# A list-scheduled trunk kernel: a re-ordered opening, later softplus, and a list model with shared ports and earlier loads

## The chip, the cores and the metric

The kernel runs on one core of a Trainium2 chip. The metric is the device time of one execution in microseconds (us); three executions of the kernel before took 1260.82, 1262.92 and 1263.37 us, the median is 1262.92 us.

## What is computed

Two layers (`DEPTH` 2) work on 256 tokens of width 1024. Cut to what matters here:

```python
for l in range(DEPTH):
    mod = silu(c) @ w_ada[l] + b_ada[l]                 # 6 * 1024 modulation values
    h = rms_norm(x, norm1_g[l]) * (1 + sc1) + sh1       # needs the first 2 * 1024 of them
    proj = h @ w_in[l]       # q, k, v, iq, ik, iw, z, xbc, dt_raw, ga, gm: 10856 columns
    o_attn = dsa_attention(rope(norm(q)), rope(norm(k)), v, rope(iq), rope(ik), iw) @ w_attn_o[l]
    dt = softplus(dt_raw + dt_bias[l])                  # one value per token and head (256 x 32)
    y = ssd_scan(silu(conv(xbc)), dt, a_log[l])
    x = x + g1 * ((sigmoid(ga) * o_attn + sigmoid(gm) * (norm(y * silu(z)) @ w_ssm_o[l])) @ w_out[l])
    x = x + g2 * conv_ffn(rms_norm(x, norm2_g[l]) * (1 + sc2) + sh2)
```

All of it is in float32. A weight product is made of three fp32r products: each weight slab is split into a rounded part `wh` and a rest `wl`, each activation into two parts in the same way.

## The kernel before, in words

**Slabs and splits.** Weights come as slabs of 4 x 128 rows by 512 columns (1 MB), loaded through the SP queue into three buffers (`st`, tag `wst`). `split_now` makes `wh` on ScalarE (ACT) and `wl = st - wh` on VectorE (DVE). A chunk of 512 output columns over 1024 rows needs two slabs. TensorE (PE) works through the chunks in the order of `plan`; between groups of products it calls `pump` (each call counts one in `slabs`), which enters small tasks from the lists `hot`, `warm`, `calm` and `cool`: the transposes, ropes, softplus, attention, scan. A task says how many pumps it waits (`later(n, ...)`) or for which tiles (`Need`).

**The static order.** Every instruction is written down once, in a fixed order for each engine, by a planner inside `trunk`. PE instructions are placed as the program comes to them, at a clock `now` that `on_pe` advances by modelled durations. Instructions of DVE, ACT, GpSimd (POOL) and the loads are entered with `give` as `Work` with a modelled duration (`takes`), and `plan_ahead` simulates all queues and picks for each engine the work that could start first (among those ready, the one entered first; `urgent` moves work ahead). `commit` then issues what starts before `now - LEAD_IN`. The modelled times decide the order only: on the chip each engine runs its list in order and waits for what it needs. In the model a load takes its bytes at 300 bytes/ns and is seen 2500 ns after its end (`HOP["dma"]`).

**Ports in the model.** A DVE `tensor_tensor` with all operands in SBUF and at least 128 elements is `heavy`: while one runs, a POOL instruction progresses at 0.18 of its speed (`CROWD`). DVE itself is never slowed.

**The opening** (`run_open`). Before layer 0 can start, the first 2048 modulation values are needed. They are made in four quarters `q`, each from two slabs of `w_ada` (`ada`, 1 MB each, five buffers of pool `op`). `ada_products` multiplies a slab with the replicated silu(c) (16 products, 32 PE instructions). Then `open_mod` runs the chain of the quarter: ACT copies the sums (`adarow`), PE transposes them, DVE adds the bias (`mod`, `amul`), and `norm_tile` makes two activation tiles `h` (DVE, ACT, DVE). With these and the quarter's slab of `w_in` four **fills** (`weigh`) can run: products for the columns of iq and k, and with two of them the narrow `misc` columns (ik, iw, dt). `modulations` is a generator that yields a `Need` ahead of each step; the loop at the end of `run_open` runs fills while the needed tile is not there by the plan's clock, but starts none within `FILL` (300 ns) of it. `warm_up(n)` writes n products of two tiles of ones into a bank that nobody reads: 10 ahead of the first modulation products, 8 after the first quarter's chain. `tables` makes the rope tables (about 25 small DVE instructions and 4 Sin on ACT) after the chain of quarter 1.

**After the opening** come the chunks Q0, V0, K1, Q1, V1, two of B and C, then the scan's inputs. The four banks of pool `pj` hold two chunks; a chunk's first product waits until its banks were read by the rope or the copy of the chunk two before.

**Softplus** (`dt_task`, in `use_misc`). When `misc` has been turned, some 26 small DVE instructions (128x64 elements) and an Exp make dt = softplus(...). The task goes to `hot` at once, and all instructions up to the polynomial's start are entered in one step. `ssd` needs its result about eight chunks later.

The queries below name line L190 for nearly everything: all instructions are issued from that one line of `commit`, so tiles tell them apart.

Of the kernel before, what the change touches and what calls it, by code (L numbers as in the profile page):

```python
# [46 lines left out]
def trunk(ctx, tc, x, c, positions, w_ada, b_ada, norm1_g, w_in, q_norm_g, k_norm_g, ssm_conv_w, ssm_conv_b,  # L47
# [13 lines left out]
    CROWD = 0.18  # L61
    ORDER = ("dve", "act", "pool", "dma", "dma_act", "dma_pool")
# [5 lines left out]
    class Work:  # L68


        __slots__ = ("key", "ns", "pr", "deps", "least", "start", "end", "done", "issue", "heavy")

        def __init__(self, key, ns, deps, least, issue):
            number[0] += 1
            self.key, self.ns, self.pr, self.deps, self.least = key, ns, number[0] - boost[0], deps, least
            self.start, self.end, self.done, self.issue, self.heavy = None, None, False, issue, False
# [36 lines left out]
    crowd_done = [0.0]  # L113

    def crowded(t, ns, until):

        if until <= t:
            return t + ns
        part = CROWD * (until - t)
        return t + ns / CROWD if ns <= part else until + ns - part  # L120

    def plan_ahead():
# [6 lines left out]
        crowd, slow = crowd_done[0], None  # L129
# [3 lines left out]
        while todo:  # L133
            best = None
            for key, ws in todo.items():
                first = None
                for w in ws[:1] if key == "dma" else ws:
                    t = w.least
                    for d in w.deps:
# [4 lines left out]
                        e += (HOP[key] if d.key[:3] != "dma" else HOP["dma"]) if d.key != key else -LAP["act"] if key == "act" else 0.0  # L144
# [5 lines left out]
                    if first is None or t < first[0]:  # L150
# [22 lines left out]
    def commit(edge=None):  # L173
# [3 lines left out]
        for key, ws in waiting.items():  # L177
            for w in sorted(ws, key=lambda w: w.start):
                if w.start < edge:
# [3 lines left out]
                    if w.heavy:  # L183
                        crowd_done[0] = w.end
# [3 lines left out]
        n = 0  # L188
# [6 lines left out]
    def end_of(w, by=None):  # L195
        if not w.done:
            plan_ahead()
        return w.end + (HOP["dma"] if w.key[:3] == "dma" else HOP[by] if by else 54.0)
# [90 lines left out]
    def give(key, outs, ins, ns, issue, least=None, heavy=False):  # L289
        deps = needs_of(outs, ins) + [w for w in behind_of if w.key == key]  # L290
        w = Work(key, ns, deps, now[0] - LEAD_IN if least is None else least, issue)
        w.heavy = heavy
# [18 lines left out]

    class Timed:
# [5 lines left out]
        def __getattr__(self, name):  # L318
            fn = getattr(self.eng, name)

            def call(*a, **k):
# [6 lines left out]
                if name.startswith(("affine", "memset")):  # L328
                    return give(self.key, outs, ins, 100.0 + 0.4 * outs[0].free_size(), issue)
                heavy = (self.key == "dve" and name == "tensor_tensor" and outs[0].free_size() >= 128  # L330
                         and not any(x.tensor._space == PSUM for x in outs + ins))
                return give(self.key, outs, ins, takes(self.key, name, outs, ins, k), issue, heavy=heavy)
# [1470 lines left out]
```

## Time and profile before

| | |
|---|---|
| median of three executions | 1262.92 us |
| the profiled execution | 1262.23 us, its span from first to last instruction 1260.5 us |
| PE busy | 1225.6 us, 97% of the span |
| DVE / ACT / POOL busy | 956.3 / 762.2 / 414.3 us |
| mean granted TensorE clock | 0.989 of 2.4 GHz |
| chain that ended last | PE 79%, DVE 12%, ACT 4%, "issue" 3%, POOL 2% |
| HBM read | 243.9 MB, 194 GB/s over the span |

Busy time of PE counts a matmul until its modelled end, and matmuls overlap, so a stretch that is busy throughout can still hold short waits. The idle time of PE and the granted clock (1.00 is 2.4 GHz, 0.50 is 1.2 GHz) tell what a stretch loses at least.

### The profile page before, as it was taken

How to read it: one execution, taken by the hardware profiler on the slowest of the kernel's cores; microseconds unless marked ns; L12 is line 12 of the kernel's file. 1: busy time of each engine (PE TensorE's matmuls, PEld its weight loads, DVE VectorE, ACT ScalarE, POOL GpSimd, SP SyncE). 2: the span in 40 equal slices, each digit the busy share in tenths (PEclk: the TensorE clock that was granted, in tenths of full speed). 3: DMA queues.
4: the chain of work that ended last, by engine and by line, in shares of the span. 5: the costliest groups of instructions: out<-in, count | busy, mean ns of one | idle time of the engine just before them, and what ended most of it. 6: DMA issues, size and time to landing. Idle time of an engine off the chain costs nothing.

```text
span 1260.5 us, 24567 instructions
## 1 busy us (share of the span) xinstructions
PE 1225.6 (97%) x9789; PEld 1140.5 (90%) x9789; DVE 956.3 (76%) x1477; ACT 762.2 (60%) x1362; POOL 414.3 (33%) x479
## 2 busy tenths in 40 slices
PE   7789999999999999999999999999999999999998
PEld 6577789999989999999997778999999999999998
DVE  4499977878786778889757997888777766678753
ACT  3356677774764357777436467877467544777742
POOL 2042533343262124564211443323304511335400
PEclk8889999999999999999989999999999999999999
DMA  9654644457456647876756455355764665566542
GB/s 300 231 182 144 209 146 171 163 193 255 159 203 215 234 156 239 276 248 229 247 180 201 148 195 193 126 170 172 240 204 153 215 236 166 181 209 202 195 162 73
DMA packets 158663, 246.53 MB, mean 196 GB/s; under 512 B 11868, under 2 KB 66870, under 8 KB 158549
## 3 DMA queue, kind: packets, MB, share of 16 engines
q1 hardware_dynamic: 157989, 244.77, 58.4%
q8 instruction: 77, 1.26, 0.4%
q14 instruction: 37, 0.30, 0.1%
q0 software_dynamic: 288, 0.19, 0.1%
q10 hardware_dynamic: 272, 0.00, 0.0%
HBM read 243.89 MB, written 1.05 MB: 194 GB/s over the span
## 4 chain that ended last, share of the span: by engine, by line
PE 79%; DVE 12%; ACT 4%; issue 3%; POOL 2%; DVEq 0%; POOLq 0%; ACTq 0%
PE bk L190 79%; DVE wl L190 4%; DVE w L190 1%; ACT wh L190 1%; DVE adacc L190 1%; DVE t L190 1%; DVE p L190 1%; POOL w L190 1%; ACT w L190 1%; ACT p L190 1%; DVE mx L190 1%; DVE ss L190 1%; DVE top L190 0%; POOL rows L190 0%; POOL rr L190 0%
## 5 line engine op out<-in xcount | busy, mean ns | idle before, releaser
L190 PE MATMUL bk<-h,wh 128*128 128x256 f32 x3488 | 646.8, 286 | 0.4 <-ACT h L190 0.4
L190 PEld LDWEIGHTS bk<-h,wh 128*128 128x128 f32 x3488 | 543.4, 192 | 12.1 <-issue 9.6
L190 DVE TENSOR_TENSOR wl<-st,wh 128x2048 fp32r<-128x2048 f32 (+1 forms) x200 | 435.0, 2179 | 146.4 <-ACT wh L190 146.0
L190 PE MATMUL bk<-h,wl 128*128 128x256 f32 x1744 | 492.0, 283 | 0.0
L190 ACT ACTIVATE wh<-st 128x2048 fp32r<-128x2048 f32 (+1 forms) x200 | 352.1, 1768 | 213.2 <-PE bk L190 176.7
L190 POOL TENSOR_TENSOR w<-w,w 128x254 f32<-128x254 f32 (+2 forms) x213 | 208.0, 992 | 416.1 <-DVE w L190 330.2
L190 PEld LDWEIGHTS bk<-h,wl 128*128 128x128 f32 x1744 | 334.1, 192 | 0.5
L190 PE MATMUL bk<-u,wh 128*128 128x256 f32 x1344 | 234.7, 279 | 0.0
L190 PEld LDWEIGHTS bk<-u,wh 128*128 128x128 f32 x1344 | 203.3, 188 | 1.6 <-issue 1.6
L190 PE MATMUL bk<-u,wl 128*128 128x256 f32 x672 | 186.1, 277 | 0.0
L190 PE MATMUL bk<-wh,h 128*128 128x512 f32 x448 | 150.4, 411 | 11.9 <-ACT wh L190 5.2
L190 ACT ACTIVATE w<-bk,vec 128x256 f32<-128x256 f32 (+2 forms) x272 | 122.2, 516 | 33.3 <-DVE w L190 19.6
L190 PEld LDWEIGHTS bk<-u,wl 128*128 128x128 f32 x672 | 126.2, 188 | 0.0
L190 DVE SCALAR_TENSOR_TENSOR adacc<-ad,chalf,adacc 128x512 f32<-128x512 f32 x140 | 121.6, 869 | 4.6 <-DMA ad<-in_w_ada_dram 4.0
L190 PEld LDWEIGHTS bk<-wh,h 128*128 128x128 f32 x448 | 83.8, 193 | 33.6 <-issue 8.0
L190 DVE SCALAR_TENSOR_TENSOR w<-bk,vec,w 128x255 f32<-128x255 f32 (+1 forms) x184 | 81.5, 475 | 16.4 <-ACT w L190 15.8
L190 PE MATMUL bk<-wl,h 128*128 128x512 f32 x224 | 90.4, 404 | 3.3 <-DVE wl L190 3.3
L190 POOL TENSOR_TENSOR u<-u,u 128x256 f32<-128x256 f32 (+1 forms) x56 | 67.3, 1219 | 57.4 <-ACT u L190 33.6
L190 POOL TENSOR_TENSOR rr<-ss,mhalf 128x16 f32<-128x16 f32 x8 | 26.0, 3254 | 98.3 <-DVE ss L190 98.3
L190 PEld LDWEIGHTS bk<-wl,h 128*128 128x128 f32 x224 | 43.4, 194 | 14.1 <-DVE wl L190 5.3
L190 ACT ACTIVATE w<-w 128x256 f32<-128x256 f32 x92 | 35.6, 412 | 30.3 <-POOL w L190 30.1
L190 ACT ACTIVATE u<-bk 128x128 f32<-128x128 f32 (+2 forms) x128 | 32.1, 325 | 30.7 <-PE bk L190 30.6
(194 smaller groups left out, 1178.5 us busy)
## 6 DMA issues: line engine op xcount, KB each, us to landing
st<-in_w_in_dram SPq DMA_DIRECT2D x80, 1024.0 KB, 5.1
st<-in_w_up_dram SPq DMA_DIRECT2D x88, 512.0 KB, 5.4
ad<-in_w_ada_dram SPq DMA_DIRECT2D x160, 256.0 KB, 5.4
st<-in_w_down_dram SPq DMA_DIRECT2D x20, 1024.0 KB, 5.3
st<-in_w_ssm_o_dram SPq DMA_DIRECT2D x16, 1024.0 KB, 5.3
st<-in_w_ada_dram SPq DMA_DIRECT2D x16, 512.0 KB, 10.2
st<-in_w_attn_o_dram SPq DMA_DIRECT2D x8, 1024.0 KB, 5.0
st<-in_w_out_dram SPq DMA_DIRECT2D x8, 1024.0 KB, 5.2
```

What stands on the lines that cost most here:

```text
L190: begun[n].issue()
```

## The change

- **The list model.** `heavy` becomes a pair `port` = (`share`, `soft`) from the new `port_of`: while a DVE instruction with `share` below 1 runs, a POOL `tensor_tensor` progresses at that share, and DVE's own end moves by `soft` times the overlap. `plan_ahead` prefers a work entered earlier if a later one would not start sooner by more than `PATIENCE` (0.2) of the later one's duration. A load is seen `EARLY` (1300 ns) after its end if that lies before 45 us, the rate is 330 instead of 300 bytes/ns up to 45 us, and the first load starts at 2.0 us. `on_pe` takes PE to be slow after a wait of over 2000 instead of 3000 ns.
- **The opening.** The two fixed `warm_up` calls go. `keep_warm(need)` puts unread products into each planned wait, ahead of fills and ahead of modulation products. Their bank is held for the whole opening. `FILL` becomes 700 ns. `tables` moves from after quarter 1's chain to after quarter 0's.
- **Softplus** is entered 44 pumps later, with more yields inside, in both layers.

```diff
+    PATIENCE = 0.2
+    EARLY = 1300.0
...
+    def landing(w):
+        return EARLY if w.end < 45000.0 else HOP["dma"]
...
-                    if first is None or t < first[0]:
+                    if first is None or t + PATIENCE * w.ns < first[0]:
...
-            if key == "pool":
-                w.end = crowded(t, w.ns, crowd)
-                slow = w
-            elif w.heavy:
-                crowd = w.end
-                if slow and slow.end > t:
-                    slow.end = crowded(t, slow.end - t, crowd)
-                    at["pool"] = max(at["pool"], slow.end - LAP["pool"])
+            if key == "pool" and w.share < 1.0:
+                w.end = crowded(t, w.ns, vec)
+                gps = w
+                if vec and not vec.done and vec.end > t:
+                    vec.end += vec.soft * (min(vec.end, w.end) - t)
+                    at["dve"] = max(at["dve"], vec.end - LAP["dve"])
+            elif key == "dve" and w.share < 1.0:
+                if gps and gps.end > t:
+                    w.end += w.soft * (min(w.end, gps.end) - t)
+                    if not gps.done:
+                        gps.end = crowded(t, gps.end - t, w)
+                        at["pool"] = max(at["pool"], gps.end - LAP["pool"])
+                vec = w
...
+    def port_of(key, name, outs, ins):
+        n = outs[0].free_size()
+        if key == "pool":
+            return (0.5, 0.0) if name == "tensor_tensor" and n >= 128 else (1.0, 0.0)
+        if key != "dve" or n < 128:
+            return 1.0, 0.0
+        if any(x.tensor._space == PSUM for x in outs + ins):
+            return 0.8, 0.0
+        if name == "tensor_tensor":
+            return 0.18, 0.1 if n > 1024 else 0.45
+        return (0.55, 0.45) if name == "scalar_tensor_tensor" else (1.0, 0.0)
...
-            give("dma", [out], [src], out.partition_size() * out.free_size() * 4 / (200.0 if now[0] < 1.0 else 300.0), issue, now[0] - 30000.0)
+            give("dma", [out], [src], out.partition_size() * out.free_size() * 4 / (250.0 if now[0] < 1.0 else 330.0 if now[0] < 45000.0 else 300.0), issue, max(2000.0, now[0] - 30000.0))
...
-        if ready > at + 3000.0:
+        if ready > at + 2000.0:
...
         misc = hold(bank())
+        spare["bank"] = hold(bank())
...
+        def keep_warm(need):
+            n = int((need.at() - now[0] - 300.0) / 225.0)
+            if n > 1:
+                warm_up(n)
...
                 if q == 1:
-                    for _ in tables():
-                        pass
                     ch["start"]()
...
                 if q == 0:
                     ahead(ch["m"], ch["m"] + 1)
-                    spare["bank"] = bank()
-                    warm_up(8)
+                if q == 0:
+                    for _ in tables():
+                        pass
...
-        warm_up(10)
         for need in modulations():
             while fills and fill_need(*fills[0]).at() < need.at() and now[0] < need.at() - FILL:
+                keep_warm(fill_need(*fills[0]))
                 fill()
+            keep_warm(need)
         ahead(ch["ada"][3][-1])
-        done(crep)
+        done(crep, spare["bank"])
...
-    FILL = 300.0
+    FILL = 700.0
...
+        DT_AFTER = 44
...
                 A.activation(e, e, AF.Exp)
+                yield
...
                 V.tensor_tensor(s2, d, d, op=ALU.mult)
+                yield
...
+                    if n % 4 == 1:
+                        yield
...
-            hot.append(dt_task())
+            hot.append(later(DT_AFTER, dt_task()))
```

## Rows read from the trace of the kernel before

**Rows 1.** The page's first part: busy us (share of the span), instructions.

```profile
PE 1225.6 (97%) x9789; PEld 1140.5 (90%) x9789; DVE 956.3 (76%) x1477; ACT 762.2 (60%) x1362; POOL 414.3 (33%) x479
```

**Rows 2.** Busy time by stretch: length, each engine (instructions), PEclk, DMA share, GB/s.

```profile
13.90:72.00 58.10, 46.76 (x412) 36.26 (x412) 27.91 (x83) 23.02 (x45) 3.95 (x13) 0.87 0.79 262
72.00:90.00 18.00, 14.42 (x60) 11.58 (x59) 17.64 (x32) 7.66 (x9) 10.39 (x5) 0.91 0.55 176
...
90.00:1260.50 1170.50, 1156.67 (x9284) 1086.39 (x9282) 904.65 (x1341) 725.82 (x1291) 391.79 (x412) 1.00 0.58 192
...
100.00:160.00 60.00, 58.66 (x350) 47.38 (x349) 58.93 (x132) 37.31 (x84) 27.03 (x25) 1.00 0.55 186
```

**Rows 3.** Waits of PE, 0 to 90 us: total us, times, longest.

```profile
PE bk L190 <- ACT wh L190: 5.2, 2, 4.1
PE bk L190 <- DVE sp_p L190: 3.6, 1, 3.6
PE bk L190 <- ACT h L190: 3.2, 2, 2.1
...
PE bk L190 <- DVE wl L190: 2.2, 3, 1.0
...
PE bk L190 <- ACT adarow L190: 0.8, 2, 0.4
```

**Rows 4.** Timeline of PE in the opening: start, us, what [idle before, releaser].

```profile
10.41 3.56 PE L190 MATMUL bk<-ones 128*128 128x128 f32 x20 [2.05 <-ACT bk L190]
...
17.08 1.95 PE L190 MATMUL bk<-ones 128*128 128x128 f32 x16
...
30.97 1.08 PE L190 MATMUL bk<-st,w 128*32 128x128 f32 x32
...
36.87 0.80 PE L190 MATMUL bk<-wh,h 128*128 128x512 f32 x1 [4.09 <-ACT wh L190]
...
58.13 1.08 PE L190 MATMUL bk<-st,w 128*32 128x128 f32 x32
...
62.00 0.50 PE L190 MATMUL bk<-wh,h 128*128 128x512 f32 x1 [2.06 <-ACT h L190]
```

**Rows 5.** One fill as a stretch; tile st's modulation loads (first, last issue) and landings.

```profile
53.43:55.29 1.86, 1.86 (x13) 1.58 (x10) 0.00 (x0) 0.00 (x0) 0.00 (x0) 1.00 0.93 330
...
L190 SPq DMA_DIRECT2D st<-in_w_ada_dram x16: 379/636/3612, 3.1 to 39.9; - x16
...
DMA to landing us min/median/max: 6.2/9.3/10.6
```

**Rows 6.** Timeline, 32 to 35 us: ACT's table load, then quarter 1's bias on DVE.

```profile
32.41 1.28 ACT L190 ACT_TABLE_LOAD   x1
...
34.16 0.22 DVE L190 TENSOR_TENSOR mod<-bk,vec 128x2 f32<-128x2 f32 x2
```

**Rows 7.** Timeline of DVE, 73 to 86 us, ahead of PE's wait for sp_p.

```profile
73.65 5.59 DVE L190 TENSOR_TENSOR wl<-st,wh 128x2048 fp32r<-128x2048 f32 x2
...
79.62 0.82 DVE L190 TENSOR_SCALAR sp_e<-sp_x 128x64 f32<-128x64 f32 x1
...
80.62 2.28 DVE L190 TENSOR_TENSOR wl<-st,wh 128x2048 fp32r<-128x2048 f32 x1
82.82 0.19 DVE L190 TENSOR_SCALAR sp_d<-sp_e 128x64 f32<-128x64 f32 x1
...
84.03 0.69 DVE L190 TENSOR_TENSOR t<-t,rr 128x512 f32<-128x512 f32 x1
84.63 0.68 DVE L190 TENSOR_TENSOR t<-bk,sint 128x512 f32<-128x512 f32 x1
```

**Rows 8.** POOL's adds of 512 columns one by one, and all wl of 2048 columns.

```profile
74.14 2.95 POOL L190 TENSOR_TENSOR t<-t,t 128x512 f32<-128x512 f32 x1
...
85.45 1.38 POOL L190 TENSOR_TENSOR t<-t,t 128x512 f32<-128x512 f32 x1 [5.06 <-issue]
...
L190 DVE TENSOR_TENSOR wl<-st,wh 128x2048 fp32r<-128x2048 f32 x176 | 417.0, 2371 | 139.5 <-ACT wh L190 139.1
```

More of the change, by code (lines that the diff above doesn't have):

```diff
@@ L68, in trunk @@
     class Work:
-        __slots__ = ("key", "ns", "pr", "deps", "least", "start", "end", "done", "issue", "heavy")
+        __slots__ = ("key", "ns", "pr", "deps", "least", "start", "end", "done", "issue", "share", "soft")
         def __init__(self, key, ns, deps, least, issue):
@@ L75, in __init__ @@
             self.key, self.ns, self.pr, self.deps, self.least = key, ns, number[0] - boost[0], deps, least
-            self.start, self.end, self.done, self.issue, self.heavy = None, None, False, issue, False
+            self.start, self.end, self.done, self.issue = None, None, False, issue
+            self.share, self.soft = 1.0, 0.0
     def region(x):
@@ L111, in writers, with crowded @@
             return [w for q, w, wrote in self.uses if wrote and meet(q, r)]
-    crowd_done = [0.0]
-    def crowded(t, ns, until):
-        if until <= t:
+    at_port = [None, None]
+    def landing(w):
+        return EARLY if w.end < 45000.0 else HOP["dma"]
+    def crowded(t, ns, by):
+        if by is None or by.end <= t:
             return t + ns
-        part = CROWD * (until - t)
-        return t + ns / CROWD if ns <= part else until + ns - part
+        part = by.share * (by.end - t)
+        return t + ns / by.share if ns <= part else by.end + ns - part
     def plan_ahead():
@@ L182, in commit @@
                     free_at[key] = max(w.start + 0.4 * w.ns, w.end - LAP[key])
-                    if w.heavy:
-                        crowd_done[0] = w.end
+                    if w.share < 1.0:
+                        at_port[key == "pool"] = w
                     begun.append(w)
@@ L287, in enter_in, with give @@
             st.uses = [u for u in st.uses if not within(u[0], r)] + [(r, w, True)]
-    def give(key, outs, ins, ns, issue, least=None, heavy=False):
+    def give(key, outs, ins, ns, issue, least=None, port=(1.0, 0.0)):
         deps = needs_of(outs, ins) + [w for w in behind_of if w.key == key]
         w = Work(key, ns, deps, now[0] - LEAD_IN if least is None else least, issue)
-        w.heavy = heavy
+        w.share, w.soft = port
         enter_in(w, outs, ins)
@@ L329, in call @@
                     return give(self.key, outs, ins, 100.0 + 0.4 * outs[0].free_size(), issue)
-                heavy = (self.key == "dve" and name == "tensor_tensor" and outs[0].free_size() >= 128
-                         and not any(x.tensor._space == PSUM for x in outs + ins))
-                return give(self.key, outs, ins, takes(self.key, name, outs, ins, k), issue, heavy=heavy)
+                return give(self.key, outs, ins, takes(self.key, name, outs, ins, k), issue, port=port_of(self.key, name, outs, ins))
             return call
@@ L951, in enter @@
         sums = w_tile("xsum", [P, 2, 2], F32, 1)
-        junk = spare["bank"] = bank(pj)
+        junk = bank(pj)
         for t, m4, xs_ in xin:
```

6 lines of the change are left out of this document (3 added, 3 removed).

## The prediction, made before the change was run

> **What bounds the kernel now.** I read the page's first part first: PE is busy 97% of 1260.5 us [rows 1], so nothing but PE's own waits, its slow clock and its unread products can be won. The stretches tell where these lie [rows 2]. Of the 34.9 us in which PE is idle (1260.5 less 1225.6), 58.10 - 46.76 = 11.3 us lie between the first modulation product and the end of the opening's products (13.9 to 72), 3.6 us in the next 18 us, 13.8 us in all the 1170.5 us after, and the rest ahead of 13.9 us. The granted clock, a mean of the levels 2.4 and 1.2 GHz, is 1.00 after 90 us to two digits, 0.87 in the opening and 0.91 from 72 to 90 us [rows 2]. The change therefore has to earn its gain in the first 90 us; after that some 14 us are left to all causes together.
>
> The waits of PE in these 90 us name what ended them [rows 3]: ACT wh 5.2 us, ACT h 3.2, DVE wl 2.2 and adarow 0.8, together 11.4 us, are the opening's; the 3.6 us on DVE sp_p are the wait at 85 us. In the timeline [rows 4] the two long ones of the opening each follow a modulation product: the quarter's chain runs and PE has no fill left to run in it. After the product at 30.97 us the next fill starts at 36.87 (4.09 us idle), after that at 58.13 us at 62.00 (2.06 us idle).
>
> Loads are not what holds the last quarter back. The last load of modulation weights is issued at 39.9 us and landings take 6.2 to 10.6 us [rows 5], so it was there between 46.1 and 50.5 us; its product starts at 58.13 [rows 4], 8 to 12 us later. PE simply reaches it late, because it stands behind fills. The order was made by a plan that is ahead of the chip: 13.34 MB of loads up to and with that slab at 300 bytes/ns and 2.5 us give 46.9 us in the plan. What PE saves ahead of 58.13 us can therefore move the end of the opening.
>
> **Part 1, the opening.** The plan's new loads give 2.0 + 13.34 MB / 330 bytes/ns + 1.3 = 43.7 us for the same slab, 3.2 us earlier than before; together with `FILL` 700 instead of 300 ns this puts the modulation products ahead of one fill or so more than before in each quarter. The fill is not lost: it is run in the chain's wait. Terms:
>
> - Waits behind a chain: 4.09 and 2.06 us idle before the first fill of quarters 1 and 3 [rows 4], and further waits for splits, 11.4 us in all [rows 3]. A fill with misc took 1.86 us [rows 5], one without has two thirds of its products; I reckon 1.5 us, and take one fill for each of the two waits, 3.0 us. Bounds 0 (the fills still stand ahead) and 6.2 (both waits covered).
> - The tables. In quarter 1's chain ACT loads a table for 1.28 us at 32.41, and DVE, in order behind the tables' instructions, adds the bias only at 34.16 [rows 6], although the sums that PE transposes were copied before that load began. Moved to quarter 0 the table load falls into ACT's time between the quarters. I take 1.3 us, bounds 0 (it then delays quarter 0's `h`) and 1.4. What it delays next is quarter 0's splits; PE's first fills wait for these (ACT wh, DVE wl of [rows 3]).
> - The clock. (1 - 0.87) x 46.76 us busy = 6.1 us lost if the low clock lay evenly [rows 2]; it follows the waits, so less. Unread products in the waits keep PE running. I take half, 3.0, bounds 0 and 6.1.
> - The unread products themselves. Twenty instructions took 3.56 us, in part at the lower clock (1.2 of 2.4 GHz), and sixteen 1.95 us at the upper [rows 4]: with two instructions each, 0.356 and 0.244 us per product, where `keep_warm` counts 0.225. The 18 that go lay in waits and so do the new ones, each wait filled up to its last 0.3 us. How much the plan fills I estimate so: from the first quarter's slabs (2.0 + 3.15 MB / 330 + 1.3 = 12.8 us) to the last it has 30.9 us; on the chip that work took 58.1 - 13.9 = 44.2 us, less some 9 us idle, 2 unread and 5 for the clock, 28 us; with about 4 us of waiting ahead of 12.8 and the plan's own optimism, 7 to 10 us are filled. Where the chip waits as planned, the overrun of 10 us is 10 x (0.244/0.225 - 1) = 0.8 us; where it has no wait at all, all 10.8 us are added. I take 1.0, nearest to the first, since the long waits stand behind chains in plan and chip alike; bounds 0 and 10.8.
> - The bank held for them leaves two of `sm` for sums, transposes and rows; each pass waits for a copy of 0.2 to 0.4 us. It hides in the time before the loads come, up to quarter 2; I take 0, bounds 0 and 1.
>
> Sum: 3.0 + 1.3 + 3.0 - 1.0 = 6.3 us earlier at the end of the opening. The bounds together are -11.8 and +13.7.
>
> **Part 2, softplus.** At 85 us PE waits for a bank that the rope of iq reads (`t<-bk,sint`, ended at 85.31), and that instruction stands on DVE behind the softplus: from 79.62 to 80.62 us and from 82.82 to 84.03 us [rows 7], 1.00 + 1.21 = 2.2 us. These go later, so the wait of 3.6 us falls to 1.4. Behind the wait the clock is low: (1 - 0.91) x 14.42 = 1.3 us [rows 2]; after 1.4 us idle I expect half of it. Gain 2.9 us, bounds 0 (another DVE instruction takes the place) and 4.9. The list has its next splits `wl` there, 2.28 us each [rows 7]; one of them ahead of the rope would undo the gain.
>
> Where softplus goes, some 60 us later, DVE is busy 58.93 of 60 us [rows 2]. It is as full as the place it leaves, the work is the same, and PE is idle there 1.3 us only, so I cost the move at 0; without that cover, 26 instructions of about 0.2 us are 5.2 us. Its readers come some eight chunks after misc, three after the new place.
>
> **Part 3, the list after the opening.** Patience and ports reorder DVE, ACT and POOL everywhere. No row shows the new order. Above, all of the 13.8 us idle after 90 us [rows 2]; I bound the gain by half of it, 7, and the loss by the same. I take 0: most single waits there are already short, and new ones can come as well as old ones go.
>
> One thing speaks against the new port model. Two `wl` ran from 73.65 to 79.24 [rows 7]; one alone takes 2.28, so the second took 3.3. POOL's add beside the first took 2.95 us, one with DVE idle at its start 1.38 [rows 8]. So POOL waited through the rest of the first `wl`, and the second `wl` waited about 1.0 us for POOL to finish. The model would lengthen that `wl` by 0.1 of the overlap, about 0.1 us. The Trainium skill, SBUF — State Buffer, "Who interferes with whom", says the same in general: the port pair shared by VectorE and GpSimd is locked for a whole instruction, and the other blocks fully. By a share model with right times part 3 could give its gain, by the lock the list stays wrong by up to 1 us at a collision, and part 3 gives nothing (1246.5 and 1253.5 us). All 176 `wl` together lose 176 x (2.371 - 2.28) = 16 us of DVE's time to this [rows 7, 8], mostly under PE's own work.
>
> **The sum.** 1262.2 us (profiled execution; 0.7 under the median of 1262.9) - 6.3 - 2.9 - 0 = 1253.0 us; against the median 1253.7. I predict 1253.5 us.
>
> **Rivals.**
>
> - **The unread products stand where the chip has no wait** (slower). The plan is ahead of the chip by 11 us at the last modulation product (46.9 against 58.1). A count of products written into the order doesn't shrink when PE comes late and the data is there: then all 10 us that the plan fills are 10.8 us of PE's time, between 10 and 58 us. With the other terms of parts 1 and 2 (3.0 + 1.3 + 3.0 + 2.9 = 10.2), less a clock term of 3.0 that is worth nothing where there was no wait, this gives 1262.9 + 10.8 - 7.2 = 1266.5. It decides from the point where the products outside real waits pass some 10 us. For it speaks that all of PE's lateness is of this kind, data before PE [rows 4, 5]; against it, that PE does wait 11.4 us in the opening [rows 3]. Chance 0.15.
> - **DVE takes the gain back.** From 72 to 160 us DVE is full [rows 2]. If PE comes earlier but DVE's splits, ropes and the moved softplus (5.2 us) don't, PE waits for `wl` there and only about 1 us is left: 1262. Against it: DVE is idle 30 us of the opening, so its work can start as much earlier as PE. Chance 0.12.
> - **The opening's end doesn't move**, since fills still stand ahead of the last modulation product or the last slab's split sets the end; only part 2 is won: 1260. Chance 0.11.
> - **The new order helps after 90 us too**: half the idle time there, 7 us: 1246.5. The lock speaks against it. Chance 0.12.
>
> **How the numbers follow.** My forecast has 0.50, with its own range 1248 to 1258.5. A measurement of this kernel tells about 0.2%, 2.5 us. Faster: 0.50 + 0.12 + 0.10 (nearly all of the unmoved opening) = 0.72. Same: 0.12 of the full DVE plus 0.01 of the unmoved opening = 0.13. Slower 0.15. The range 1245 to 1263.5 holds the forecast, the helped rest, the unmoved opening and the full DVE, with their tails, and leaves out the rival on the other side.
>
> **What would show it.** Right: the modulation product now at 58.13 us starts at about 52, the two long waits behind chains shrink to under 2 us, the clock of 13.9 to 72 us is 0.93 or more, and the wait at 85 us is gone or under 1.5 us at a place some 6 us earlier. Wrong: the last modulation product stays at 58 us or later with tens of `ones` products ahead of it; a new wait of PE for `wl` or a rope between 75 and 160 us; idle time of PE after 90 us over 18 us.

## The result, and the profile after

The changed kernel took 1255.83 us (median of four runs, 1255.38 to 1256.02), the kernel before 1262.55 us in the runs beside them: a ratio of 0.9948, 95% interval 0.9931 to 0.9965, or 6.6 us less. The profiled execution's span is 1254.1 us.

The page's first part, then the same stretches as in [rows 2] (length, busy us and instructions of PE, PEld, DVE, ACT and POOL, granted clock, DMA share, GB/s):

```profile
PE 1229.6 (98%) x9881; PEld 1145.8 (91%) x9881; DVE 972.5 (78%) x1477; ACT 764.2 (61%) x1362; POOL 462.6 (37%) x479
```

```profile
13.90:72.00 58.10, 55.58 (x520) 45.93 (x513) 32.57 (x76) 25.72 (x46) 12.56 (x15) 1.00 0.79 260
72.00:90.00 18.00, 16.57 (x81) 13.22 (x80) 16.78 (x21) 9.21 (x24) 11.40 (x10) 1.00 0.67 216
90.00:1254.10 1164.10, 1148.65 (x9241) 1078.84 (x9239) 915.14 (x1345) 722.01 (x1274) 430.49 (x405) 1.00 0.58 192
100.00:160.00 60.00, 58.91 (x375) 49.28 (x375) 56.65 (x129) 36.73 (x81) 30.89 (x26) 1.00 0.56 186
```

PE is idle 1254.1 - 1229.6 = 24.5 us, where it was 34.9. The opening's part fell from 11.3 to 58.10 - 55.58 = 2.5 us, that of the next 18 us from 3.6 to 1.4; after 90 us it rose by 1.6 us (1164.10 - 1148.65 = 15.45 against 13.83). The clock of both early stretches is 1.00 (0.87 and 0.91 in [rows 2]). Against these gains stand 92 more PE instructions (9881 against 9789): unread products. POOL, with the same 479 instructions, is busy 48 us longer [rows 1].

PE's waits between 13.9 and 72 us (total us, times, longest), and its timeline in the opening and behind it (start, us, what, idle before and releaser):

```profile
PE bk L201 <- DVE wl L201: 1.4, 3, 1.0
PE bk L201 <- ACT wh L201: 1.1, 1, 1.1
```

```profile
9.21 4.21 PE L201 MATMUL bk<-ones 128*128 128x128 f32 x18 [1.10 <-DVE xt L201]
...
14.48 2.72 PE L201 MATMUL bk<-ones 128*128 128x128 f32 x22
...
18.91 5.30 PE L201 MATMUL bk<-ones 128*128 128x128 f32 x46
...
52.11 1.08 PE L201 MATMUL bk<-st,w 128*32 128x128 f32 x32
...
57.41 0.50 PE L201 MATMUL bk<-wh,h 128*128 128x512 f32 x1 [1.09 <-ACT wh L201]
58.95 0.50 PE L201 MATMUL bk<-wl,h 128*128 128x512 f32 x1 [1.03 <-DVE wl L201]
...
77.10 0.70 PE L201 MATMUL bk<-wh,h 128*128 128x512 f32 x2
...
82.15 0.73 PE L201 MATMUL bk<-wh,h 128*128 128x512 f32 x2 [1.13 <-DVE t L201]
```

The last modulation product moved from 58.13 to 52.11 us, and the two long waits behind chains (4.09 and 2.06 us in [rows 4]) have become two of 1.1 and 1.0 us. The product of `wh` and `h` that waited 3.58 us for softplus and started at 85.46 us now starts at 77.10 with no idle time ahead of it; a few products on, a smaller wait of 1.13 us for a rope has appeared. The row of the kernel before:

```profile
85.46 0.70 PE L190 MATMUL bk<-wh,h 128*128 128x512 f32 x2 [3.58 <-DVE sp_p L190]
```

DVE's timeline in that place shows why: `sp_x`, the input of softplus, is read out of the bank, and then the rope and the next split follow at once.

```profile
74.94 0.28 DVE L201 TENSOR_TENSOR sp_x<-bk,dtb 128x32 f32<-128x32 f32 x2
75.13 0.68 DVE L201 TENSOR_TENSOR t<-t,rr 128x512 f32<-128x512 f32 x1
75.73 0.68 DVE L201 TENSOR_TENSOR t<-bk,sint 128x512 f32<-128x512 f32 x1
76.33 2.28 DVE L201 TENSOR_TENSOR wl<-st,wh 128x2048 fp32r<-128x2048 f32 x1
78.53 1.78 DVE L201 TENSOR_TENSOR t<-t,rr 128x512 f32<-128x512 f32 x1
```

**A scale for all kernels.** The products with a `wl` operand are 2704 in every kernel. From the traces I take the start of the n-th of them, and subtract the start of the n-th one in the kernel before: negative is earlier. Other PE work can be placed before or after it, so single values wander, but a level that stays is time won or lost. The columns are named by the time in the kernel before: 65.6 us is the opening's end, 463.7 the second norm of layer 0, 680.2 the start of layer 1's chunks, 891.8 to 1104.8 holds its scan. One profiled execution stands behind each row, and it need not lie at the kernel's median: that of `list_only` was 3.9 us under it, at the highest granted clock of its twelve runs (1258.83 to 1266.26 us), that of `soft_l0` 3.3 us over it, the others within 1.9 us. `soft_only` has the order of the kernel before up to 79 us and still shows -0.8 at 65.6 us, so one execution alone tells no difference of this size.

| kernel | 65.6 | 112.7 | 463.7 | 680.2 | 891.8 | 1104.8 | 1232.8 |
|---|---|---|---|---|---|---|---|
| the change | -5.2 | -9.9 | -8.6 | -10.2 | -10.1 | -7.1 | -6.4 |
| open_only | -5.8 | -4.1 | -4.1 | -4.2 | -4.1 | -4.1 | -4.1 |
| soft_only | -0.8 | -5.2 | -3.4 | -4.4 | -6.3 | -5.3 | -5.3 |
| list_only | -4.3 | -7.6 | -5.1 | -7.8 | -6.9 | -3.9 | -3.9 |
| open_soft | -5.4 | -7.3 | -4.8 | -6.3 | -8.2 | -8.3 | -8.3 |
| quiet | -2.8 | -6.7 | -5.5 | -7.1 | -7.0 | -3.9 | -1.8 |
| no_soft | -5.5 | -5.3 | -6.2 | -3.9 | -0.7 | +1.7 | +1.7 |
| soft_l0 | -5.8 | -9.4 | -8.1 | -11.2 | -3.6 | -2.7 | -2.1 |
| os_loads | -6.7 | -10.8 | -6.9 | -7.0 | -8.9 | -9.0 | -9.0 |
| os_ports | -5.3 | -9.1 | -2.2 | -5.9 | -7.2 | +3.7 | +3.7 |
| os_patience | -2.8 | -6.0 | -2.6 | +2.4 | +4.3 | +5.3 | +11.1 |
| os_lock | -5.4 | -13.0 | +4.1 | +1.5 | -2.6 | +6.9 | +7.0 |
| oldports | -7.2 | -11.0 | -6.8 | -0.3 | +1.5 | +2.6 | +9.9 |

The change has won 9.9 us by 112.7 us, more than it ends with. Some 3 us are lost again in layer 1's scan. The other kernels with the whole new list lose there too: `quiet` 3.1 us, `list_only` 3.0, `no_soft` 2.4, `soft_l0` 0.9.

### The profile page after: what moved, and what is told of

It is laid out like the page before. It is cut to its first block, busy times and chain, and to the rows that moved or that the text cites. A ratio compares the mean times of both kernels' runs of the same rounds, so it can differ in the third digit from the quotient of the medians.

```text
span 1254.1 us, 24710 instructions
## 1 busy us (share of the span) xinstructions
PE 1229.6 (98%) x9881; PEld 1145.8 (91%) x9881; DVE 972.5 (78%) x1477; ACT 764.2 (61%) x1362; POOL 462.6 (37%) x479
## 4 chain that ended last, share of the span: by engine, by line
PE 83%; DVE 11%; ACT 2%; issue 2%; POOL 2%; DMA 0%; DVEq 0%; ACTq 0%; POOLq 0%
PE bk L201 83%; DVE wl L201 3%; ACT wh L201 1%; DVE p L201 1%; DVE w L201 1%; DVE t L201 1%; DVE mx L201 1%; DVE adacc L201 1%; POOL rr L201 1%; DVE u L201 1%; ACT w L201 1%; POOL t L201 0%; DVE top L201 0%; POOL rows L201 0%; DVE ss L201 0%
## 5 line engine op out<-in xcount | busy, mean ns | idle before, releaser
L201 DVE TENSOR_TENSOR wl<-st,wh 128x2048 fp32r<-128x2048 f32 (+1 forms) x200 | 440.0, 2207 | 87.6 <-ACT wh L201 87.4
L201 POOL TENSOR_TENSOR w<-w,w 128x254 f32<-128x254 f32 (+2 forms) x213 | 248.9, 1180 | 375.9 <-DVE w L201 252.8
L201 PE MATMUL bk<-wh,h 128*128 128x512 f32 x448 | 147.0, 403 | 2.2 <-DVE t L201 1.1
L201 DVE SCALAR_TENSOR_TENSOR w<-bk,vec,w 128x255 f32<-128x255 f32 (+1 forms) x184 | 84.2, 477 | 26.4 <-ACT w L201 24.9
L201 POOL TENSOR_TENSOR u<-u,u 128x256 f32<-128x256 f32 (+1 forms) x56 | 63.5, 1154 | 50.1 <-ACT u L201 30.7
L201 POOL TENSOR_TENSOR rr<-ss,mhalf 128x16 f32<-128x16 f32 x8 | 31.6, 3947 | 75.7 <-DVE ss L201 75.6
L201 PEld LDWEIGHTS bk<-wl,h 128*128 128x128 f32 x224 | 42.4, 189 | 12.2 <-DVE wl L201 3.8
L201 ACT ACTIVATE p<-bk,acs 128x256 f32<-128x256 f32 (+1 forms) x128 | 43.4, 423 | 9.3 <-PE bk L201 8.6
```

Source lines behind the costliest of these rows:

```text
L201: begun[n].issue()
```

## The experiments

Ratios are to the kernel before, which was run again beside each batch (medians 1261.53 to 1262.55 us), with 95% intervals; differences in us are (ratio - 1) x 1262.6.

**The parts one by one.** The first three kernels put one part of the change each into the kernel before.

`open_only`, the opening alone:

```diff
+        spare["bank"] = hold(bank())
...
+            keep_warm(need)
...
-    FILL = 300.0
+    FILL = 700.0
```

Expected: 

> The kernel before with the change's opening alone (keep_warm, the held bank, FILL 700, tables after quarter 0); list model, load model and softplus as before. My theory (the opening wins by its own order and by unread products in its waits): the last modulation product starts at 51 to 55 us instead of 58.1, the granted clock from 13.9 to 72 us is above 0.95, and the time is 4 to 6 us under the kernel before, 1256.5 to 1258.5 us. Rival (the new load times lead the opening's order, without them fills still stand ahead): the last modulation product stays at 57 to 59 us and the time within 1.5 us of before.

Measured: 1257.32 us, ratio 0.9968 (0.9956 to 0.9979), 4.0 us less. The last modulation product starts at 51.79 us with the load times of before, and the clock of 13.9 to 72 us is 0.97, so the theory held and the rival, that the new load times lead, fell. The opening ends 5.8 us earlier, but PE then stands longer in softplus's shadow. That product, PE's wait for softplus, and the stretch behind the opening:

```profile
51.79 1.08 PE L190 MATMUL bk<-st,w 128*32 128x128 f32 x32
```

```profile
PE bk L190 <- DVE sp_p L190: 3.6, 1, 3.6
```

```profile
72.00:90.00 18.00, 14.45 (x59) 11.48 (x58) 17.52 (x39) 5.73 (x16) 8.61 (x6) 0.81 0.66 213
```

The wait for softplus is as long as it was [rows 3], and the granted clock of the stretch is 0.81 instead of 0.91 [rows 2]: of the 5.8 us 1.7 are given back there, and the table stays at -4.1 to the end. The opening's gain and the softplus move are not independent.

`soft_only`, the later softplus alone:

```diff
+        DT_AFTER = 44
...
-            hot.append(dt_task())
+            hot.append(later(DT_AFTER, dt_task()))
```

Expected: 

> The kernel before with the change's softplus alone (44 pumps later, more yields, both layers). My theory (layer 0's rope of iq no longer waits): PE's wait of 3.6 us at 85 us is under 2 us, 2 to 4 us under the kernel before. New theory from the run without the softplus part (it cost about 10 us where 3 were expected, most of it behind the second layer's start): layer 1 gains as well, 4 to 8 us under the kernel before in all. Rival (the move pays only under the new list): within 1.5 us of before.

Measured: 1256.51 us, ratio 0.9958 (0.9946 to 0.9971), 5.3 us less. PE's wait behind the opening is 2.0 us, for a rope, instead of 3.6. By the table some 3 us of it are there by 463.7 us; between 463.7 and 891.8 us, in layer 1, another 2.9 come (1.0 of the whole goes again by 1104.8). The prediction counted only layer 0.

`list_only`, the list model alone:

```diff
-                    if first is None or t < first[0]:
+                    if first is None or t + PATIENCE * w.ns < first[0]:
...
-        if ready > at + 3000.0:
+        if ready > at + 2000.0:
```

Expected: 

> The kernel before with the change's list model alone (ports, patience, load times, slow threshold); opening and softplus as before. My theory (the list gives nothing or costs some): 0 to 3 us over the kernel before, 1262.5 to 1265.5 us, with POOL's busy time up by tens of us as in the changed kernel (462.6 against 414.3 us). Rival (the list model is a gain that the moved softplus hides): 2 us or more under the kernel before.

Measured: 1262.71 us, ratio 1.0014 (1.0001 to 1.0027), 1.8 us more: a small loss, of which the interval leaves 0.1 to 3.4 us. POOL is busy 463.6 us, as expected. In the profiled execution the last modulation product starts early here too, with the opening code of before:

```profile
53.06 1.08 PE L201 MATMUL bk<-st,w 128*32 128x128 f32 x32
```

So the new list alone moves it by 5.1 us, the new opening alone by 6.3 (51.79 us), and both together by 6.0 (52.11 us): they win the same time. What `list_only` wins in the opening is taken back later (-7.6 at 112.7 us, -3.9 at the end).

**Two parts together.** `open_soft` is the change without its list model:

```diff
-                    if first is None or t + PATIENCE * w.ns < first[0]:
+                    if first is None or t < first[0]:
...
-                return give(self.key, outs, ins, takes(self.key, name, outs, ins, k), issue, port=port_of(self.key, name, outs, ins))
+                return give(self.key, outs, ins, takes(self.key, name, outs, ins, k), issue, heavy=heavy)
```

Expected: 

> The changed kernel without its list model (ports, patience, load times, slow threshold as before), opening and softplus as in the change. My theory (the list gives nothing or costs some): 7 to 10 us under the kernel before, so 0.5 to 3 us under the changed kernel. Rival (the list carries part of the gain): 4 to 5 us under the kernel before, 1.5 us or more over the changed kernel.

Measured: 1253.52 us, ratio 0.9931 (0.9919 to 0.9943), 8.7 us less; the parts alone give 4.0 + 5.3 = 9.3. Its median is 2.3 us under the change's, though the two intervals overlap. In the table it gains next to nothing in layer 1's scan and loses nothing there (-8.2, -8.3), while the change goes from -10.1 to -7.1.

`no_soft` is the change without the later softplus:

```diff
-            hot.append(later(DT_AFTER, dt_task()))
+            hot.append(dt_task())
```

Expected: 

> The changed kernel without its softplus part: the task is entered at once and with the old yields. My theory (softplus stands ahead of the rope of iq on DVE): PE's wait ahead of the chunk V0, at about 77 to 81 us, is 3 to 4 us instead of 1.3, and the time 2 to 4 us over the changed kernel, 1258 to 1260 us. Rival (the new list order finds a place for it): within 1 us of the changed kernel.

Measured: 1264.51 us, ratio 1.0027 (1.0015 to 1.0039), or 10 us over the change. I had expected 2 to 4. PE's wait at 85 us does not come back in its old place. Softplus's small steps make a split late instead, a few microseconds on:

```profile
88.74 0.79 PE L201 MATMUL bk<-wl,h 128*128 128x512 f32 x1 [3.42 <-DVE wl L201]
```

The rest is lost in layer 1 (-6.2 at 463.7, +1.7 at 1104.8).

**The terms.** `quiet` asks what the unread products are worth. The plan counts them at their places as the change does, so the order on every engine is the change's, but they are not issued. It leaves out only products that nobody reads.

```diff
-                warm_up(n)
+                for _ in range(n):
+                    on_pe(spare["bank"][:, 0:P], ones, ones, lambda: None)
```

Expected: 

> The changed kernel with the same order on every engine, but without the 64 unread products of the opening's waits (the plan counts them, none is issued). My theory (they pay by the clock): the granted clock from 13.9 to 72 us falls to 0.85 to 0.93 and the opening's end comes 2 to 4 us later, time 1258 to 1260 us. Rival (the order alone wins, and the products only fill real waits): within 1 us of the changed kernel, or up to 3 us under it where they stand outside real waits.

Measured: 1259.91 us, ratio 0.9985 (0.9976 to 0.9995), 4.7 us over the change. Its opening as a stretch, and PE's waits in it:

```profile
13.90:72.00 58.10, 47.81 (x372) 36.02 (x371) 29.66 (x80) 24.16 (x46) 7.23 (x14) 0.94 0.80 263
```

```profile
PE bk L201 <- ACT wh L201: 5.1, 3, 2.7
PE bk L201 <- DVE wl L201: 4.1, 4, 1.3
```

Without them PE is idle 58.10 - 47.81 = 10.3 us of the stretch, with them 2.5 us. Over 0 to 72 us it is 16.8 against 7.6 us, so some 9 of the 17.2 us that the products take lie where PE would have waited.

The 0.94 in the row is too high. The trace of `quiet` has no record of the clock before 26.8 us, and the column counts such time as 1.00. The rows show the lower level until then: the first fill's product of 0.79 us is as long as the one of 0.80 us at 36.87 us in the kernel before [rows 4], where the granted clock is 0.50 (35.5 to 42.3 us); in the change it takes 0.48. This product and the modulation product behind the fill, in `quiet` and then in the change:

```profile
21.02 0.79 PE L201 MATMUL bk<-wh,h 128*128 128x512 f32 x1 [2.68 <-ACT wh L201]
...
25.63 1.65 PE L201 MATMUL bk<-st,w 128*32 128x128 f32 x32
```

```profile
23.96 0.48 PE L201 MATMUL bk<-wh,h 128*128 128x512 f32 x1
...
25.88 1.08 PE L201 MATMUL bk<-st,w 128*32 128x128 f32 x32
```

With the lower level up to 26.8 us, and in the two later stretches of 3.4 us that the trace records, the mean from 13.9 to 72 us is about 0.83, an estimate, a little under the range of the theory. In the change the instructions on `ones` take 0.23 us each in the group at 9.21 us and 0.12 in the next two, and its first record of the upper level is at 13.7 us.

So in the first quarter the products cost time and give it back at once. They make the copy of the sums 1.5 us later (16.81 us in `quiet`, 18.28 in the change, whose second modulation product starts only at 17.13 us, behind 22 instructions on `ones`) and the first fill 2.9 us later. That fill with its waits then takes 4.6 us in `quiet` and 1.9 in the change, and by the next modulation product the change is 0.25 us behind.

The end of the opening is 2.4 us earlier with the products than without (-5.2 against -2.8). At 112.7 us the lead is 3.2 us, and it is still 3.2 at 1104.8: with the same order on every engine, a lead of the opening stays. Of the rest of the 4.7, 1.4 us come behind 1104.8 us (-7.1 to -6.4 in the change, -3.9 to -1.8 in `quiet`), where the order is the same; I don't put these down to the products.

`soft_l0` moves softplus in layer 0 alone:

```diff
-        DT_AFTER = 44
+        DT_AFTER = 44 if l == 0 else 0
```

Expected: 

> The changed kernel with softplus moved in layer 0 only; in layer 1 it is entered at once (with the new yields). Theory from the run without the softplus part (layer 1's move is worth more than layer 0's): 4 to 8 us over the changed kernel, lost between the start of layer 1 (about 650 us) and 740 us. Rival (the loss there was the chance of one order, not softplus): within 2 us of the changed kernel.

Measured: 1258.89 us, ratio 0.9979 (0.9970 to 0.9988), 3.9 us over the change, just under the range of the theory and at the place that it named. Layer 1 now has a wait like layer 0's before. PE's timeline, then DVE's ahead of that wait:

```profile
697.70 1.22 PE L201 MATMUL bk<-wh,h 128*128 128x512 f32 x2 [4.96 <-DVE t L201]
```

```profile
694.55 0.21 DVE L201 SCALAR_TENSOR_TENSOR sp_p<-sp_x,sp_p 128x64 f32<-128x64 f32 x1
...
696.37 0.68 DVE L201 TENSOR_TENSOR t<-bk,tc 128x512 f32<-128x512 f32 x1
```

The rope that frees PE's bank comes on DVE right behind softplus and the top-k steps mixed with it. In the table 7.6 us go between 680.2 and 891.8 us, part of which comes from work placed otherwise.

**The list model taken apart.** `open_soft` came out under the change and `list_only` over the kernel before, so something in the list seems to cost. `oldports` takes the new ports out of the change and leaves patience and load times in:

```diff
-        if name == "tensor_tensor":
-            return 0.18, 0.1 if n > 1024 else 0.45
-        return (0.55, 0.45) if name == "scalar_tensor_tensor" else (1.0, 0.0)
+        heavy = (key == "dve" and name == "tensor_tensor" and outs[0].free_size() >= 128
+                 and not any(x.tensor._space == PSUM for x in outs + ins))
+        return (0.18, 0.0) if heavy else (1.0, 0.0)
```

Expected: 

> The changed kernel with the port model of before (only a DVE tensor_tensor in SBUF slows POOL, nothing slows DVE); patience and load times as changed. My theory (the share model makes DVE and POOL collide more often): POOL's busy time falls from 462.6 to about 415 us, DVE's from 972.5 to about 957, and the time is 0 to 3 us under the changed kernel. Rival (the ports are a gain): 1.5 us or more over the changed kernel. If POOL's busy time stays, patience is what moves the collisions.

Measured: 1272.32 us, ratio 1.0089 (1.0072 to 1.0105), 18 us over the change where I had expected a little under it. POOL's busy time falls to 447.7 us, not to 415. A plain miss, and the reason for the next four kernels, which add one piece at a time to `open_soft`.

`os_ports`:

```diff
+            elif key == "dve" and w.share < 1.0:
+                if gps and gps.end > t:
+                    w.end += w.soft * (min(w.end, gps.end) - t)
```

Expected: 

> The kernel open_soft (opening and softplus of the change, list model of the kernel before) with one part of the list model added: the new shares at the ports (port_of, DVE slowed by POOL), patience 0, old load times. Theory, the ports bring more collisions of DVE and POOL (POOL's busy time rose to 462 us with them): 1 to 4 us over open_soft (1253.5), with POOL busy over 440 us. Rival, chance of one order: within 2 us of open_soft and POOL's busy time moves as it likes.

Measured: 1264.38 us, ratio 1.0028 (1.0017 to 1.0039), 12.2 us over `open_soft`. Neither theory holds: the loss is far larger than both say, and POOL is busy 425.9 us, near `open_soft`'s 423.3. Eleven of the 12 us go between 891.8 and 1104.8 us, which holds layer 1's scan. PE's waits from 950 to 1070 us, in `os_ports` and then in `open_soft`:

```profile
PE bk L201 <- DVE h L201: 2.0, 1, 2.0
PE bk L201 <- DVE xdt L201: 2.0, 1, 2.0
PE bk L201 <- ACT xdt L201: 1.2, 1, 1.2
PE bk L201 <- ACT h L201: 1.1, 1, 1.1
```

```profile
PE bk L190 <- POOL rr L190: 0.5, 1, 0.5
PE bk L190 <- ACT h L190: 0.2, 1, 0.2
```

These are 6.3 us for steps of the scan that come late on DVE and ACT (the 0.5 us for POOL's `rr` is in both), and two stretches of 3.4 us at a granted clock of 0.50, at 1009 and 1046 us, which `open_soft` doesn't have there.

`os_patience`:

```diff
-                    if first is None or t < first[0]:
+                    if first is None or t + 0.2 * w.ns < first[0]:
```

Expected: 

> open_soft with only the preference for work entered earlier (PATIENCE 0.2), ports and load times of the kernel before. Theory, patience is what costs and the new ports mend most of it: 5 to 15 us over open_soft (as the full change with the old ports came out 16 us over the full change), with waits of PE for adacc, adarow or POOL's w in the second half of the kernel. Rival, those 16 us were the chance of one order: within 3 us of open_soft.

Measured: 1275.85 us, ratio 1.0106 (1.0091 to 1.0121), 22 us over `open_soft`. The sign and the names of the waits are as expected, the size is above the range, and most of the waits for `adacc` come before 650 us, in the first half. PE's waits after 90 us:

```profile
PE bk L190 <- DVE adacc L190: 5.7, 4, 2.0
PE bk L190 <- ACT adarow L190: 3.6, 1, 3.6
PE bk L190 <- POOL w L190: 2.9, 3, 1.4
```

Here is POOL's longer busy time, too. Its adds of 256 columns in the groups view (count, busy us, mean ns, idle before and what ended it), in `open_soft`, `os_patience` and the change:

```profile
L190 POOL TENSOR_TENSOR w<-w,w 128x256 f32<-128x256 f32 x77 | 90.8, 1186 | 123.5 <-ACT w L190 61.7 <-DVE w L190 61.1
```

```profile
L190 POOL TENSOR_TENSOR w<-w,w 128x256 f32<-128x256 f32 x77 | 108.3, 1412 | 89.5 <-ACT w L190 61.4 <-DVE w L190 27.0 <-DVE mod L190 0.4
```

```profile
L201 POOL TENSOR_TENSOR w<-w,w 128x256 f32<-128x256 f32 x77 | 118.7, 1547 | 94.7 <-ACT w L201 66.8 <-DVE w L201 27.1
```

With patience 0.2 the same 77 adds take 1412 and 1547 ns instead of 1186. `os_ports`, with the new ports and no patience, has 1172; `oldports`, with patience and the old ports, 1412. So the longer adds come with patience; the new ports lengthen them only on top of it.

`os_loads`:

```diff
+        return EARLY if w.end < 45000.0 else HOP["dma"]
...
-        if ready > at + 3000.0:
+        if ready > at + 2000.0:
```

Expected: 

> open_soft with only the new load times (seen 1300 ns after their end up to 45 us, 330 bytes/ns, first load at 2.0 us) and the slow clock after 2000 ns. Theory, nothing is behind loads in the opening but more planned fills and fewer unread products: within 1.5 us of open_soft, and the last modulation product within 1 us of 52 us. Rival, the plan runs further ahead of the chip and fewer unread products stand in the opening: 1 to 4 us over open_soft with a granted clock under 0.95 from 13.9 to 72 us.

Measured: 1252.55 us, ratio 0.9929 (0.9917 to 0.9940), the lowest of all and not to be told from `open_soft`, as expected. The last modulation product starts at 50.26 us, earlier than the expected 51 to 53. At 112.7 us it is 3.5 us ahead of `open_soft`, at 463.7 2.1, at the end 0.7: in another order most of such a lead is gone by the end, where between `quiet` and the change it stayed.

`os_lock` gives the plan a port model by what the rows show, in which the two engines take turns whole. The edit goes further than its expectation says: it holds `scalar_tensor_tensor`, `tensor_scalar` and copies on SBUF tiles to the turns as well.

```diff
+            if key == "pool" and w.share < 1.0:
+                w.end = max(t, vec.end if vec else t) + w.ns
+                gps = w
+            elif key == "dve" and w.share < 1.0:
+                w.end = max(t, gps.end if gps else t) + w.ns
+                vec = w
```

Expected: 

> open_soft with a port model by what the rows show: DVE's tensor_tensor between SBUF tiles and POOL's tensor_tensor take turns whole, neither starts before the other ends; patience 0, old load times. Theory, an order that knows the turns has fewer stretched instructions: POOL busy at or under 415 us, mean of the 2048-column wl at or under 2.35 us, and a time 0 to 4 us under open_soft. Rival, the collisions lie under PE's own work and the plan's order moves the time by chance only: within 2 us of open_soft to either side, whatever POOL's busy time does.

Measured: 1269.28 us, ratio 1.0064 (1.0050 to 1.0078), 16.8 us over `open_soft`; POOL is busy 453.4 us and the mean of the 2048-column `wl` 2.384 us. My theory fell on all three. A model made after these rows did not give a better order.

## Why the prediction was right, and where it was lucky

I predicted 1253.5 us and faster; 1255.83 came out. The direction and the places in the first 90 us were right. The sum came within 2.3 us because errors of size partly cancelled: the opening and the list were taken too well, softplus not well enough.

- **The opening, 6.3 us predicted.** The end of the opening is 5.2 us earlier, and alone in the kernel before the part is worth 4.0 us at the end. The order that I forecast came: modulation products ahead of fills (52.11 us against a forecast of about 52), chain waits of 1.1 us, clock 1.00. I had put it down to the plan's new load times together with `FILL`; `open_only` shows that the load times aren't needed for it, and `list_only`, in its one profiled execution, that `FILL` isn't. By its terms:
  - Waits and tables, 3.0 + 1.3: `quiet` gains 2.8 us without the new products, but it also lacks the 18 old ones and has the new list, and no run has these two terms alone. The tables' share was well sized: ACT's table load has gone to 12.08 us, ahead of the first modulation product (the row below), and quarter 1's bias on DVE starts 2.07 us after its modulation product (32.31 less 30.24) instead of 3.19 [rows 4, 6], 1.1 us sooner. Quarter 0's first `h` starts 2.1 us after its copy of the sums, before 2.2, so the lower bound I gave did not come true. If 1.1 us are the tables', some 1.7 of `quiet`'s 2.8 are left for the waits, where I had 3.0; that is an estimate.
  - Clock less unread products, 3.0 - 1.0 = 2.0: `quiet` shows a net 2.4 us at the opening's end and 3.2 at 112.7. That the net came out near is luck, for both terms were too small. The cost is 2.9 us at the first fill, so what the products give back is about 5.3. My estimate of how much the plan fills (7 to 10 us) was well under, too: the plan's count is 64 x 0.225 = 14.4 us, and the five groups of `ones` take 17.2 us.
  - What was not in the sum: if the opening ends earlier and softplus stays, 1.7 us go again behind it.

```profile
12.08 1.28 ACT L201 ACT_TABLE_LOAD   x1
```

- **Softplus, 2.9 us predicted.** Layer 0 was right: about 3 us in `soft_only`, and the wait at 85 us is gone. It started 8.4 us earlier instead of some 6, opening and softplus together. The mis-sized term is the layer count. The change sits in both layers, and I read the wait in layer 0 alone; in the kernel before no wait of PE in layer 1 names softplus. `soft_only` shows about 2.9 us there and `soft_l0` 3.9. The wait at 697.7 us in `soft_l0` shows how softplus costs in the new order; which step loses the 2.9 us in the kernel before is not shown. Measured alone the part is worth 5.3 us, taken out of the change 10.
- **The list after the opening, 0 predicted, bounds 7 to either side.** By the whole time the list cost about 2 us: 1.8 in `list_only` (0.1 to 3.4), 2.1 from `open_soft` to the change, whose intervals overlap. Behind 112.7 us it cost more: there the change loses 3.5 us of its lead and `open_soft` gains 1.0, after the list had won 2.6 us up to that point. The place is layer 1's scan, where the change goes from -10.1 to -7.1 us. Two waits there make 2.7 of the 3 us, and each stands behind a split that ACT was given ahead of a short step PE needs. PE's timeline of the change, then ACT's:

```profile
1001.88 0.84 PE L201 MATMUL bk<-xdt,wh 128*128 128x256 f32 x2 [1.22 <-ACT xdt L201]
...
1037.30 0.84 PE L201 MATMUL bk<-h,wh 128*128 128x256 f32 x2 [1.47 <-ACT h L201]
```

```profile
999.61 1.92 ACT L201 ACTIVATE wh<-st 128x2048 fp32r<-128x2048 f32 x1 [0.59 <-PE bk L201]
1001.43 0.40 ACT L201 ACTIVATE xdt<-u 128x256 fp32r<-128x256 f32 x1
...
1035.03 1.91 ACT L201 ACTIVATE wh<-st 128x2048 fp32r<-128x2048 f32 x1 [2.58 <-DVE h L201]
1036.85 0.71 ACT L201 ACTIVATE h<-u 128x256 fp32r<-128x256 f32 x2
```

In `open_soft` PE's waits of this stretch were 0.5 and 0.2 us (above).

Put together from the parts alone: 4.0 + 5.3 - 1.8 = 7.5 us, measured 6.6 together. I had 6.3 + 2.9 - 0 = 9.2. That the parts nearly add up does not make them independent: the new list and the new opening win the same time, and softplus is worth 5.3 or 10 us depending on the order around it.

**The rivals.** Unread products outside real waits: true of about half of them, for 2.9 us at the first fill, and refuted as the sign of the whole by `quiet`, which is slower without them. DVE taking the gain back: no, PE is idle 1.1 us of the busy stretch from 100 to 160 us, less than before [rows 2], though some of the early lead does go (9.9 us at 112.7, 8.6 at 463.7). An opening whose end stays: refuted by the start at 52.11 us. A better order after 90 us: refuted; PE's idle time there rose by 1.6 us. One of the signs that I had named for wrong did come, a new wait for a rope between 75 and 160 us: the 1.13 us at 82.15 us. It is a third of the wait that it follows, and PE's idle time from 72 to 90 us still fell from 3.6 to 1.4.

**The port argument.** I had said that a share model is wrong by up to 1 us at a collision, and that the list would therefore give nothing. The first half stands, the second is not what the runs show. POOL's add that begins beside the split in the change, and one that begins with DVE idle:

```profile
76.54 3.21 POOL L201 TENSOR_TENSOR t<-t,t 128x512 f32<-128x512 f32 x1 [3.83 <-DVE t L201]
...
82.23 1.29 POOL L201 TENSOR_TENSOR t<-t,t 128x512 f32<-128x512 f32 x1 [2.48 <-issue]
```

The first starts at 76.54 us. The split of the DVE rows above ends at 76.33 + 2.28 = 78.61, and 1.14 us later, at 79.75, the add is done; the second takes 1.29. (The add of 1.38 us in [rows 8], which I had called one with DVE idle at its start, began together with a 0.23 us step on `sp_p`.) DVE's `t<-t,rr`, begun at 78.53, ends at 80.31, 0.56 us after the add; alone it takes 0.69 [rows 7]. Each runs when the other has finished. The Trainium skill, SBUF — State Buffer, "Who interferes with whom", calls the shared port pair an exclusive lock, but describes the whole-instruction hold for VectorE's 2-port modes, a condition that I had left out; of a `tensor_tensor` with both inputs in SBUF it says only that it contends with GpSimd's reads. The rows show whole turns for that instruction too. But `os_lock`, which plans with such turns, is 16.8 us slower than `open_soft`. So how near the port model comes to the rows does not decide which order is faster here: the old shares are in the two fastest kernels, and in the change the new ones are worth 18 us against them (`oldports`).

**What stays open.** Why patience alone costs 22 us, ports alone 12, and both with the load times only 2. Each late step can be read from its trace, as above. That the change's values of patience and shares balance each other by a mechanism was not shown, and other values were not tried. What the runs do show is that four orders from another list model (`oldports`, `os_ports`, `os_patience`, `os_lock`) lie 12 to 22 us over `open_soft`, with their losses in different places, while `os_loads` lies level with it and the change 2 us over it.

## What to carry to other kernels

Where one engine is busy 97% of the time, look for its idle time and its low clock by stretch, and size a change there; then ask for each moved step how often it occurs, since the second layer held about half of softplus's gain without one wait in its name. Filling planned waits with unread products paid here, although about half of them stood outside real waits; a kernel with the same order and without them is the clean test. Check a clock column against the durations of equal instructions before you use it. Treat the list model of a static order as a risk of its own: without its ports and patience this change is at 1252.6 to 1253.5 us (`os_loads`, `open_soft`), 2 us under it by the medians though not outside the intervals, and neither of the two other port models tried on `open_soft` improved on that.

## What the runs showed of the hardware that was not expected

DVE and POOL `tensor_tensor` instructions on SBUF tiles took turns whole to within 0.2 us, as the rows of 76.33 to 80.31 us show (1.14 us behind the split against 1.29 alone, 0.56 behind the add against 0.69).

A wait of PE of 2.06 us was followed by a lower granted clock, waits of 1.1 us in the same place were not. In `open_only` the first product behind the last quarter's chain starts at 56.63 us (a shorter wait of 0.56 us follows), and from 58.6 us PE runs at the lower level. In the change the waits of 1.09 and 1.03 us at 57.41 and 58.95 us were followed by no fall: the clock is 1.00 up to 90 us.

```profile
56.63 0.50 PE L190 MATMUL bk<-wh,h 128*128 128x512 f32 x1 [2.06 <-ACT h L190]
```

```profile
58.60:62.10 3.50, 3.50 (x11) 2.87 (x11) 2.73 (x2) 1.13 (x2) 0.00 (x0) 0.51 0.53 159
```
